# Decay series to the start, codes by GpSimd, two row sets by VectorE, unit splits to the end of the drain

## The chip, the cores and the metric

One core of a Trainium2 chip runs one layer of a decoder trunk for 256 tokens of 2048 features. The core has five engines, each with its own instruction queue, worked off in program order: TensorE (PE in the profile; its weight loads are PEld), VectorE (DVE), ScalarE (ACT), GpSimd (POOL) and SyncE (SP), which here only issues DMAs. An instruction waits at the head of its queue until what it needs is there, and everything behind it waits with it. The metric is the device time of one execution in microseconds, the median of the timed runs.

## The reference, cut to what matters

```python
z    = rmsnorm(h, norm1_g)
proj = z @ w_in                        # 1024 pool | 1024 x-branch | 1024 gate columns
xc   = causal depthwise conv4(x branch)
r, i = sigmoid(xc @ gate_a_w + b), sigmoid(xc @ gate_x_w + b)     # per head, 8 heads
log_a = (LRU_C * r) * log_sigmoid(lru_lambda)                     # the decay
a, b = exp(log_a), sqrt(-expm1(2 * log_a)) * (i * xc)
y    = concat(pool_mixer(pool columns), associative_scan(a, b) * gelu(gate))
h    = h + y @ w_out
# PEER: 8 heads, 16 of 128 x 128 = 16384 single-neuron experts each
z2   = rmsnorm(h, norm2_g);  q = z2 @ peer_wq
top 16 of (q . keys1) + (q . keys2)    # an expert's number is i1 * 128 + i2
act  = gelu(peer_u[expert] . z2);  w = softmax(top scores) * act
out  = rmsnorm(h + sum over the 128 chosen experts of w * peer_v[expert], norm_f_g)
```

## The kernel before, in words

**Stages.** Time runs through five of them. (1) Projections: `z` is transposed and normed, and 24 column blocks of `w_in` are multiplied, each followed over the next steps by its mixer work. (2) The output projection, the second norm and the queries. (3) The U stage: the first 1536 of the 2048 features are multiplied densely, all 16384 rows of `peer_u` by all 256 tokens, 64 pairs of row blocks with three units each; the scores stay on chip in `sw`. The last 512 features are gathered per chosen expert by GpSimd's indirect DMAs and dotted on VectorE. (4) The drain: for each token the 128 chosen scores are picked out of `sw` (extract), run through GELU and the softmax weights, and spread again into a 128 x 128 map of weights per token, written back into `sw` (form). (5) The V stage: the map times all rows of `peer_v`, densely for 1536 features, with gathers for the other 512; then residual and last norm.

**Units and splits.** Every weight comes in units of 128 x 1024 floats (512 KB). `Stream` (L68) holds them: `load` (L94) issues a unit's DMA on SP into a free raw buffer, `split` (L103) makes a high part on ScalarE (`hi`, L109) and the rest on VectorE (`lo`, L110), which frees the raw buffer, and `take` (L130) hands both to three matmuls per product (L359 to L361, L1107 to L1109). There are three raw and two high/low buffer pairs, more of either in some stages. `give_back` (L126) frees the pair used last.

**Projections and steps.** `Steps` (L138) is a plan by hand: `steps.at(k, f)` runs `f` k ticks later, two ticks to a column block. The plan at L336 to L344 sets the first norm, the splits of the gate weights and, at ticks 6, 8 and 9, the decay series. `decay_1` (L309) takes Abs and Exp of `lru_lambda`'s column on ScalarE, adds 2 on GpSimd and prepares four small rows of pooling divisors there (`inv`); `decay_2` (L317) takes two reciprocals on VectorE; `decay_3` (L321) sums a series of 27 GpSimd operations on 128 x 8 values and leaves the two scales `l8` and `l8n`, which are first used in `s10` (L433). GpSimd also computes `cl`, the low part of the convolved x branch (`pool_rest`, L261, called in `s4`, L411), which TensorE needs for the gate products in `s6` (L415).

**The drain.** The loop at L1116 runs n from 0 to 38 over groups of eight tokens, and its program order is the order on every engine. In iteration n it extracts group n (`extract_mm`, L987: code matmuls that mask by i2, then matmuls of the one-hot of i1 with `sw`; VectorE's maximum over 128 is the pick, L1001), forms group f = n - 6 (`form_mm`, L1064) and evacuates group f - 1 into `sw` on ScalarE (`form_out`, L1071). The one-hots of i1 for extracts (`onehot_t`, L870) come from GpSimd mostly, from index rows loaded by SP (`load_ib`, L866). A form needs two row sets of 8 x 128 per token group. `one` (L1029) is the one-hot of i1: on ScalarE eight Abs and a Relu (L1038, L1041), on VectorE one comparison (L1034); `O1_BY` and `O1_LAST` say which, the last six groups alternating ScalarE and VectorE. `two` (L1056) compares with i2 and multiplies by the weights on VectorE; `two_pool` (L1046) does one or two of the eight rows on GpSimd. Both sets have two buffers, so set k + 2 waits until form k has been read. The sets of the first groups go into unit buffers that are free by then (`early`, `early2`), and ScalarE builds the first three in iterations 0 to 2. Every fourth iteration runs a GELU over 32 tokens: VectorE (`gelu_1`), ScalarE's Square (`gelu_1s`, L1014), VectorE (`gelu_2`), ScalarE's Tanh (`gelu_2s`, L1023), VectorE (`gelu_3`, L1027), which writes the weights `wt`. The forms of a block cannot begin before that.

**Codes.** Before the extracts, tables of the chosen experts' i2 bits come back from DRAM: `code_tile` (L903) issues four DMAs of 8 KB on SP for two groups, three tiles ahead of the drain and the others inside it.

**The V stage's start.** At n = 9 the first three value units are loaded; at n = 14 and 18 (`V_SPLIT`) a unit is split and the next one loaded. At n = 33 and 34 TensorE does the first half of the products of value units 0 and 1 (`v_mm`, L1101).

Of the kernel before, what the change touches and what calls it, by code (L numbers as in the profile page):

```python
# [10 lines left out]
F32 = mybir.dt.float32  # L11
# [9 lines left out]
T = 256  # L21
# [27 lines left out]
NCB, V_LOAD, V_SPLIT = 3, 9, (14, 18)  # L49
# [109 lines left out]
def kernel(ctx: ExitStack, tc: tile.TileContext, x, cols, front, gates_w, keys, u1, u2, v1, v2,  # L159
# [60 lines left out]
    warm = cst.tile([128, 1], F32, name="warm")  # L220
    nc.vector.memset(warm, 1.0)
    nc.scalar.activation(warm, warm, AF.Sqrt)
    for c in range(4):
        if c == 2:
            st.load()
        for i in range(2):
            nc.sync.dma_start(xh[:, i, c * 512:(c + 1) * 512], x[i, :, c * 512:(c + 1) * 512])
    while st.load():
        pass
    graw = []  # L230
    for i in range(2):
        raw = fp.tile([128, 1024], F32, name="b8", tag="b8", bufs=3)
        nc.sync.dma_start(raw, gates_w[i])
        graw.append(raw)
    g2b = xpool.tile([128, D2], F32, name="g2b")
    gw = []

    nc.sync.dma_start(g2b, g2row.partition_broadcast(128))
    def split_gates(i):
        hi = fp.tile([128, 8, 128], F32R, name=f"gwh{i}")  # L240
        lo = fp.tile([128, 8, 128], F32R, name=f"gwl{i}")
        nc.scalar.activation(hi.rearrange("p a b -> p (a b)"), graw[i], AF.Copy)
        nc.gpsimd.tensor_tensor(lo.rearrange("p a b -> p (a b)"), graw[i],
                                hi.rearrange("p a b -> p (a b)").bitcast(F32), op=OP.subtract)
        gw.append((hi, lo))

    def rsqrt(dst, ss, scr):

        v, s, a = scr
        nc.vector.tensor_scalar(v, ss, 1.0 / D, EPS, op0=OP.mult, op1=OP.add)  # L250
        nc.scalar.activation(s, v, AF.Sqrt)
        nc.vector.reciprocal(s, s)
        nc.vector.tensor_tensor(a, s, s, op=OP.mult)
        nc.vector.tensor_tensor(a, a, v, op=OP.mult)
        nc.vector.tensor_scalar(a, a, -0.5, 1.5, op0=OP.mult, op1=OP.add)
        nc.vector.tensor_tensor(dst, s, a, op=OP.mult)

    def pool_mul(o, a, b):
        nc.gpsimd.tensor_tensor(o, a, b, op=OP.mult)

    def pool_rest(o, a, hi):  # L261
        nc.gpsimd.tensor_tensor(o, a, hi.bitcast(F32), op=OP.subtract)

    zhi, zlo = z_tiles()

    def to_z(k, srcs, gcol, zh, zl, p=None):

        p = bank("tp", 2) if p is None else p
        for i in range(2):
            nc.tensor.transpose(p[:, i * 128:(i + 1) * 128], srcs[i][:, k * 128:(k + 1) * 128], ident)  # L270
        nc.scalar.activation(zh[k], p[:, :T], AF.Copy, scale=gcol)
        nc.vector.scalar_tensor_tensor(zl[k], p[:, :T], gcol, zh[k].bitcast(F32), op0=OP.mult, op1=OP.subtract)

    def bcast_t(dst, v):

        p = bank("tp", 2)
        for i in range(2):
            nc.tensor.transpose(p[:, i * 128:(i + 1) * 128], v[:, i:i + 1].to_broadcast([128, 128]), ident)
        nc.scalar.activation(dst, p[:, :T], AF.Copy)

    def z1(k):
        tag, n = (("tp", 2), ("sm", 2), ("mm", 4), ("tp", 2), ("sm", 2), ("mm", 4), ("tp", 2), ("sm", 2))[k // 2]
        to_z(k, (xh[:, 0, :], xh[:, 1, :]), col("g1", k), zhi, zlo, bank(tag, n))


# [7 lines left out]
    jx = fp.tile([128, 2, D], BF, name="jx", tag="b8", bufs=3)[:, :, :512]  # L293
    ss1c = fp.tile([128, 2, 4], F32, name="ss1c")

    def square_x(c):
        cs = slice(c * 512, (c + 1) * 512)
        nc.scalar.activation(jx[:, 0, :], xh[:, 0, cs], AF.Square, accum_out=ss1c[:, 0, c:c + 1])
        nc.vector.scalar_tensor_tensor(jx[:, 1, :], xh[:, 1, cs], 1.0, xh[:, 1, cs], op0=OP.mult, op1=OP.mult,
                                       accum_out=ss1c[:, 1, c:c + 1])  # L300

    def first_norm():
        nc.vector.tensor_reduce(ss1, ss1c, AX.X, OP.add)
        rsqrt(rstd1, ss1, [fp.tile([128, 2], F32, name=f"rq{j}") for j in range(3)])
# [30 lines left out]

    steps.at(0, lambda: square_x(2))  # L336
# [5 lines left out]
    steps.at(6, decay_1)  # L342
    steps.at(8, decay_2)
    steps.at(9, decay_3)  # L344
# [567 lines left out]
    for pr in range(64):  # L912
        acc = [bank("mm", 4) for _ in range(2)]
        for kg in range(GU):
# [15 lines left out]
            if u == nu - DOT_END + 1:  # L930
# [5 lines left out]
                prepare_codes()  # L936
                ibt = zbpool.tile([128, 2, 8, 128], BF, name="ibt", tag="zbhi")
# [420 lines left out]
```

## Time and profile before

| | |
|---|---|
| median of 3 runs | 1629.93 us (1625.88 to 1631.35) |
| the profiled execution's own time | 1624.22 us |
| its span, first to last instruction | 1622.2 us |
| TensorE busy | 1570.7 us, 97% of the span |
| VectorE, GpSimd, ScalarE busy | 83%, 58%, 54% |
| projections to the end of queries | 0 to 340 us |
| U stage | 340 to 929 us, TensorE busy over 98% of it |
| drain | 929 to 1084 us, TensorE busy 139.75 of 155 us |
| V stage | 1084 to 1600 us, then the last norm |

Times inside an execution are microseconds from the span's start. A row of the timeline gives start, duration, engine, line, operation, tile written and tiles read, shapes and how many instructions were merged into it; in brackets stands how long the engine had been idle before it and what released it. The granted clock is a share of TensorE's full rate.

### The profile page before, as it was taken

How to read it: one execution, taken by the hardware profiler on the slowest of the kernel's cores; microseconds unless marked ns; L12 is line 12 of the kernel's file. 1: busy time of each engine (PE TensorE's matmuls, PEld its weight loads, DVE VectorE, ACT ScalarE, POOL GpSimd, SP SyncE). 2: the span in 40 equal slices, each digit the busy share in tenths (PEclk: the TensorE clock that was granted, in tenths of full speed). 3: DMA queues.
4: the chain of work that ended last, by engine and by line, in shares of the span. 5: the costliest groups of instructions: out<-in, count | busy, mean ns of one | idle time of the engine just before them, and what ended most of it. 6: DMA issues, size and time to landing. Idle time of an engine off the chain costs nothing.

```text
span 1622.2 us, 28967 instructions
## 1 busy us (share of the span) xinstructions
PE 1570.7 (97%) x10734; PEld 1452.3 (90%) x10734; DVE 1347.1 (83%) x2297; ACT 881.1 (54%) x1223; POOL 941.1 (58%) x754
## 2 busy tenths in 40 slices
PE   8899999999999999999999989989999999999996
PEld 8899888999999999999999989977888888888885
DVE  7799755899999998777777479978899898989897
ACT  6675545444444445444444568874555555555554
POOL 2476201266677778555554269866676666666663
PEclk9999999999999999999999999999999999999998
DMA  7455666578988889998998423129999999999992
GB/s 255 145 169 180 207 199 203 160 237 274 329 299 292 274 302 333 324 314 306 311 309 296 135 88 118 48 69 315 308 336 366 331 334 362 358 330 334 350 322 99
DMA packets 124973, 418.60 MB, mean 258 GB/s; under 512 B 18128, under 2 KB 20720, under 8 KB 124704
## 3 DMA queue, kind: packets, MB, share of 16 engines
q1 hardware_dynamic: 82528, 278.70, 52.2%
q0 software_dynamic: 42304, 138.06, 24.0%
q8 instruction: 84, 1.38, 0.4%
q14 instruction: 57, 0.47, 0.1%
HBM read 411.90 MB, written 4.78 MB: 257 GB/s over the span
## 4 chain that ended last, share of the span: by engine, by line
PE 76%; DVE 10%; ACT 6%; DMA 5%; issue 2%; POOL 1%; SPq 0%; ACTq 0%; DVEq 0%; POOLq 0%
PE mm L361 14%; PE mm L360 13%; PE mm L359 13%; PE acc L1108 9%; PE acc L1109 9%; PE acc L1107 9%; DVE lo L110 3%; DMA raw<-in_v_dram 2%; DVE sw L694 2%; PE mm L585 2%; PE mm L583 2%; PE mm L584 2%; ACT ott L1038 2%; DMA raw<-in_u_dram 1%; DVE sw L714 1%
## 5 line engine op out<-in xcount | busy, mean ns | idle before, releaser
L109 ACT ACTIVATE hi<-raw 128x1024 fp32r<-128x1024 f32 x390 | 413.1, 1059 | 470.9 <-PE mm L360 200.9
L110 DVE TENSOR_TENSOR lo<-raw,hi 128x1024 fp32r<-128x1024 f32 x390 | 495.4, 1271 | 176.6 <-ACT hi L109 171.7
L361 PE MATMUL mm<-zahi,lo 128*128 128x256 f32 x2016 | 572.6, 284 | 6.7 <-DVE lo L110 6.5
L359 PE MATMUL mm<-zahi,hi 128*128 128x256 f32 x2016 | 573.4, 284 | 0.0
L360 PE MATMUL mm<-zalo,hi 128*128 128x256 f32 x2016 | 571.3, 283 | 0.0
L1189 POOL DMA_INDIRECT gatv<-in_v_dram,e x256 | 327.0, 1277 | 179.4 <-DVE accg L1199 121.8
L361 PEld LDWEIGHTS mm<-zahi,lo 128*128 128x128 f32 x2016 | 387.5, 192 | 8.8 <-DVE lo L110 8.5
L359 PEld LDWEIGHTS mm<-zahi,hi 128*128 128x128 f32 x2016 | 387.8, 192 | 0.2
L360 PEld LDWEIGHTS mm<-zalo,hi 128*128 128x128 f32 x2016 | 387.7, 192 | 0.0
L684 POOL DMA_INDIRECT sw<-in_u_dram,e x128 | 160.6, 1254 | 90.9 <-DVE sw L694 39.1
L1107 PE MATMUL acc<-hi,wht 128*128 128x512 f32 x512 | 199.5, 390 | 1.7 <-ACT wht L1095 1.7
L1108 PE MATMUL acc<-lo,wht 128*128 128x512 f32 x512 | 199.7, 390 | 0.3 <-DVE lo L110 0.2
L1109 PE MATMUL acc<-hi,wlt 128*128 128x512 f32 x512 | 199.4, 389 | 0.0
L1199 DVE SCALAR_TENSOR_TENSOR accg<-gatv,wtok,accg 128x512 f32<-128x512 f32 x252 | 183.4, 750 | 3.3 <-DMA gatv<-in_v_dram,e 3.3
L1107 PEld LDWEIGHTS acc<-hi,wht 128*128 128x128 f32 x512 | 96.1, 188 | 21.9 <-ACT wht L1095 1.9
L1108 PEld LDWEIGHTS acc<-lo,wht 128*128 128x128 f32 x512 | 96.1, 188 | 21.7 <-DVE lo L110 1.9
L1109 PEld LDWEIGHTS acc<-hi,wlt 128*128 128x128 f32 x512 | 96.1, 188 | 20.0 <-DVE wlt L1096 0.4
L684 POOL DMA_INDIRECT gatp<-in_u_dram,e x64 | 74.2, 1160 | 55.9 <-DVE gatp L694 45.6
L684 POOL DMA_INDIRECT gatl<-in_u_dram,e x64 | 72.8, 1138 | 54.1 <-DVE gatl L694 43.4
L1108 PE MATMUL acc<-more,wht 128*128 128x512 f32 x256 | 100.1, 391 | 1.4 <-DVE more L110 1.4
L1107 PE MATMUL acc<-more,wht 128*128 128x512 f32 x256 | 99.7, 389 | 0.4 <-ACT more L109 0.4
L694 DVE SCALAR_TENSOR_TENSOR sw<-sw,zg 128x512 f32<-128x512 f32 x128 | 98.2, 786 | 2.0 <-DMA sw<-in_u_dram,e 2.0
(300 smaller groups left out, 2576.1 us busy)
## 6 DMA issues: line engine op xcount, KB each, us to landing
raw<-in_u_dram SPq DMA_DIRECT2D x192, 512.0 KB
raw<-in_v_dram SPq DMA_DIRECT2D x125, 512.0 KB
raw<-in_front_dram SPq DMA_DIRECT2D x114, 512.0 KB
sw<-in_v_dram SPq DMA_DIRECT2D x67, 512.0 KB
ibt<-i_dram SPq DMA_DIRECT2D x32, 256.0 KB
gatv<-in_v_dram,e POOLq DMA_INDIRECT x256, 5.9
xh<-in_x_dram SPq DMA_DIRECT2D x8, 256.0 KB
h_dram<-xh POOLq DMA_DIRECT2D x8, 256.0 KB, 4.7
```

The lines of the kernel that those rows point to most:

```text
L109: nc.scalar.activation(s[1], r[1], AF.Copy)
L110: nc.vector.tensor_tensor(s[2], r[1], s[1].bitcast(F32), op=OP.subtract)
L359: nc.tensor.matmul(o, ah, bh, start=first, stop=False)
L360: nc.tensor.matmul(o, ah, bl, start=False, stop=False)
L361: nc.tensor.matmul(o, al, bh, start=False, stop=last)
L684: nc.gpsimd.indirect_dma_start(out=g, out_offset=None, in_=u2, in_offset=bass.IndirectOffsetOnAxis(ap=e32[:, i, sl:sl + 1], axis=0))
L694: nc.vector.scalar_tensor_tensor(g, g, 1.0, zg[:, i, :], op0=OP.mult, op1=OP.mult, accum_out=sg[:, i, sl:sl + 1])
L1107: nc.tensor.matmul(banks[c][i], whi[:, j, ts], vh[:, s], start=first, stop=False)
L1108: nc.tensor.matmul(banks[c][i], whi[:, j, ts], vl[:, s], start=False, stop=False)
L1109: nc.tensor.matmul(banks[c][i], wlo[:, j, ts], vh[:, s], start=False, stop=last)
L1189: nc.gpsimd.indirect_dma_start(out=g, out_offset=None, in_=v2, in_offset=bass.IndirectOffsetOnAxis(ap=e32[:, i, s:s + 1], axis=0))
L1199: nc.vector.scalar_tensor_tensor(a, g, wtok[:, i, s:s + 1], a, op0=OP.mult, op1=OP.add)
```

## The change

- `decay_1` and `decay_2` are called before everything else that uses ScalarE and VectorE, ahead of the `warm` memset and its Sqrt (their definitions move up unchanged, with the tiles they use); `decay_3` is called once the first loads are issued. Ticks 6, 8 and 9 are empty of them.
- The first three code tiles are issued on GpSimd's queue, two right after their buffers are cleared (twelve units before the end of the U stage), the third after its own is cleared. Later tiles stay on SP.
- The row sets of groups 0 and 1 are compared on VectorE at the last unit of the U stage, where it already builds three sets of the other kind. ScalarE builds the third in iteration 0.
- The Square of the first GELU block is issued ahead of the extract of its iteration.
- From n = 32 on, ScalarE's row sets (28 and 30) are issued one iteration earlier, at n = 32 and n = 34.
- The two unit splits go from n = 14 and 18 to n = 33 and 35, after the last step of a GELU, and the first value products from n = 33 and 34 to 35 and 37.

```diff
-NCB, V_LOAD, V_SPLIT = 3, 9, (14, 18)
+NCB, V_LOAD, V_SPLIT = 3, 9, (33, 35)
...
     st.limit = n_v
+    lamc = colt[:, COLS["lam"]]
+    lt = [fp.tile([128, 8], F32, name=f"lt{j}") for j in range(4)]
...
+    decay_1()
+    decay_2()
     warm = cst.tile([128, 1], F32, name="warm")
     nc.vector.memset(warm, 1.0)
     nc.scalar.activation(warm, warm, AF.Sqrt)
...
     nc.sync.dma_start(g2b, g2row.partition_broadcast(128))
+    decay_3()
...
-    steps.at(6, decay_1)
-    steps.at(8, decay_2)
-    steps.at(9, decay_3)
...
-    def code_tile(k):
+    def code_tile(k, eng=nc.sync):
         for q in range(4 * k, min(4 * k + 4, T // 4)):
             g = q % 4
-            nc.sync.dma_start(code_buf[k % NCB][32 * g:32 * g + NCODE],
+            eng.dma_start(code_buf[k % NCB][32 * g:32 * g + NCODE],
...
                 prepare_codes()
+                code_tile(0, nc.gpsimd)
+                code_tile(1, nc.gpsimd)
...
                 nc.gpsimd.memset(code_buf[2], 0.0)
+                code_tile(2, nc.gpsimd)
             if u >= nu - 7 and st.loaded == n_v and not codes_out:
                 codes_out.append(u)
-                for k in range(NCB):
-                    code_tile(k)
                 for k in (2, 3):
                     load_ib(k)
             if u == nu - 1:
...
+                early = [by8(v) for e in (st.hl_free[0], st.hl[st.used - 1]) for v in e[1:]][:O1_EARLY]
+                for k in range(2):
+                    nc.vector.tensor_tensor(early[k], *rows(i1t, k), op=OP.is_equal)
...
         if gelu:
             gelu_1(b)
+            if b == 0:
+                gelu_1s(b)
...
-        g1s = (lambda: gelu_1s(b)) if gelu else lambda: None
+        g1s = (lambda: gelu_1s(b)) if gelu and b else lambda: None
         if 0 <= f + 1 < NP:
             two(f + 1)
-        if O1_EARLY <= f + 1 < NP:
+        by_act = lambda k: O1_LAST[k % 2] == "a"
+        if O1_EARLY <= f + 1 < NP and not (n > NP and by_act(f + 1)):
             one(f + 1, g1s)
         else:
             g1s()
+        if n >= NP and f + 2 < NP and by_act(f + 2):
+            one(f + 2)
...
-        if n < O1_EARLY:
-            one(n)
+        if n == 0:
+            one(O1_EARLY - 1)
...
+        if gelu:
+            gelu_3(b)
         if n in V_SPLIT:
             st.give_back()
             st.split()
             st.load()
-        if gelu:
-            gelu_3(b)
...
-        if n in (NP + 1, NP + 2):
-            c = n - NP - 1
+        if n in (NP + 3, NP + 5):
+            c = (n - NP - 3) // 2
             v_mm(0, c, 0, *st.hl[st.used + c][1:])
```

More of the change, by code (lines that the diff above doesn't have):

```diff
@@ L219 @@
     st.limit = n_v
[L220 to L283, printed above, removed]
     rstd1 = fp.tile([128, 2], F32, name="rstd1")
@@ L291, with pool_mul @@
     inv = fp.tile([128, 4, 16], F32, name="inv")
[L293 to L304, printed above, removed]
+    def pool_mul(o, a, b):
+        nc.gpsimd.tensor_tensor(o, a, b, op=OP.mult)
     lamc = colt[:, COLS["lam"]]
@@ L334, in decay_3 @@
         pool.tensor_scalar(l8n, lt[3], -LRU_C * 0.5, None, op0=OP.mult)
+    decay_1()
+    decay_2()
+    warm = cst.tile([128, 1], F32, name="warm")
+    nc.vector.memset(warm, 1.0)
+    nc.scalar.activation(warm, warm, AF.Sqrt)
+    for c in range(4):
+        if c == 2:
+            st.load()
+        for i in range(2):
+            nc.sync.dma_start(xh[:, i, c * 512:(c + 1) * 512], x[i, :, c * 512:(c + 1) * 512])
+    while st.load():
+        pass
+    graw = []
+    for i in range(2):
+        raw = fp.tile([128, 1024], F32, name="b8", tag="b8", bufs=3)
+        nc.sync.dma_start(raw, gates_w[i])
+        graw.append(raw)
@@ new lines, in rsqrt, with pool_rest @@
+    def rsqrt(dst, ss, scr):
+        v, s, a = scr
+        nc.vector.tensor_scalar(v, ss, 1.0 / D, EPS, op0=OP.mult, op1=OP.add)
+        nc.scalar.activation(s, v, AF.Sqrt)
+        nc.vector.reciprocal(s, s)
+        nc.vector.tensor_tensor(a, s, s, op=OP.mult)
+        nc.vector.tensor_tensor(a, a, v, op=OP.mult)
+        nc.vector.tensor_scalar(a, a, -0.5, 1.5, op0=OP.mult, op1=OP.add)
+        nc.vector.tensor_tensor(dst, s, a, op=OP.mult)
+    def pool_rest(o, a, hi):
+        nc.gpsimd.tensor_tensor(o, a, hi.bitcast(F32), op=OP.subtract)
@@ new lines, with to_z, bcast_t @@
+    zhi, zlo = z_tiles()
+    def to_z(k, srcs, gcol, zh, zl, p=None):
+        p = bank("tp", 2) if p is None else p
+        for i in range(2):
+            nc.tensor.transpose(p[:, i * 128:(i + 1) * 128], srcs[i][:, k * 128:(k + 1) * 128], ident)
+        nc.scalar.activation(zh[k], p[:, :T], AF.Copy, scale=gcol)
+        nc.vector.scalar_tensor_tensor(zl[k], p[:, :T], gcol, zh[k].bitcast(F32), op0=OP.mult, op1=OP.subtract)
+    def bcast_t(dst, v):
+        p = bank("tp", 2)
+        for i in range(2):
+            nc.tensor.transpose(p[:, i * 128:(i + 1) * 128], v[:, i:i + 1].to_broadcast([128, 128]), ident)
+        nc.scalar.activation(dst, p[:, :T], AF.Copy)
@@ new lines, in z1, with square_x @@
+    def z1(k):
+        tag, n = (("tp", 2), ("sm", 2), ("mm", 4), ("tp", 2), ("sm", 2), ("mm", 4), ("tp", 2), ("sm", 2))[k // 2]
+        to_z(k, (xh[:, 0, :], xh[:, 1, :]), col("g1", k), zhi, zlo, bank(tag, n))
+    jx = fp.tile([128, 2, D], BF, name="jx", tag="b8", bufs=3)[:, :, :512]
+    ss1c = fp.tile([128, 2, 4], F32, name="ss1c")
+    def square_x(c):
+        cs = slice(c * 512, (c + 1) * 512)
+        nc.scalar.activation(jx[:, 0, :], xh[:, 0, cs], AF.Square, accum_out=ss1c[:, 0, c:c + 1])
+        nc.vector.scalar_tensor_tensor(jx[:, 1, :], xh[:, 1, cs], 1.0, xh[:, 1, cs], op0=OP.mult, op1=OP.mult,
+                                       accum_out=ss1c[:, 1, c:c + 1])
@@ L336, with first_norm @@
+    def first_norm():
+        nc.vector.tensor_reduce(ss1, ss1c, AX.X, OP.add)
+        rsqrt(rstd1, ss1, [fp.tile([128, 2], F32, name=f"rq{j}") for j in range(3)])
     steps.at(0, lambda: square_x(2))
@@ L973 @@
     o1s, o2s = (ott[:, 0], ott[:, 1]), (ott[:, 2], ohtt[:, 2])
-    early = [by8(v) for e in (st.hl_free[0], st.hl[st.used - 1]) for v in e[1:]][:O1_EARLY]
     def o1(n, read=False):
```

10 lines of the change are left out of this document (added).

## The prediction

> **What bounds the kernel now.** I read the times by stage first, then what TensorE (PE) waited for, then the three stages that the change touches in order of time. Columns of the stretches: length, busy time of each engine with its instructions, granted clock, DMA share, GB/s.
>
> ```profile
> 50.00:55.30 5.30, 0.36 (x4) 0.16 (x2) 2.70 (x5) 1.06 (x1) 4.54 (x13) 0.72 0.65 191
> 55.30:59.20 3.90, 3.85 (x18) 3.86 (x19) 1.36 (x3) 1.44 (x3) 1.37 (x2) 0.51 0.04 14
> 948.00:952.20 4.20, 4.13 (x24) 4.13 (x24) 3.61 (x5) 0.00 (x0) 4.08 (x2) 0.50 0.23 70
> 1010.00:1057.00 47.00, 44.72 (x422) 43.31 (x421) 44.82 (x51) 39.50 (x96) 36.31 (x14) 1.00 0.20 54
> 1057.00:1084.00 27.00, 19.56 (x157) 17.91 (x156) 20.56 (x26) 20.66 (x43) 17.24 (x13) 1.00 0.00 1
> 1160.00:1600.00 440.00, 440.00 (x1941) 363.76 (x1940) 397.32 (x440) 231.68 (x218) 279.02 (x220) 1.00 0.94 331
> ```
>
> PE sets the end: in the long value stage (1160 to 1600) it is never idle, so what is saved ahead of that stage moves the end by as much, unless its loads come too late. It stands still at few places; the waits are total, times, longest:
>
> ```profile
> PE tp L360 <- POOL cl L262: 5.0, 1, 5.0
> PE exb L991 <- DVE asw L1001: 4.8, 1, 4.8
> ```
>
> ```profile
> PE fob L1067 <- ACT ott L1041: 4.0, 4, 1.7
> PE fob L1067 <- DVE ott L1034: 3.9, 2, 2.0
> ```
>
> One is in the projection near 50 us, three are in the drain (929 to 1084). After each of the first two the clock is granted at half (0.51, 0.50) for some 4 us. The drain's last part is a chain between four engines, none of them full.
>
> **The change part by part.** Sums go against the profiled execution: 1624.22 us, its span 1622.2. It lies 5.7 us under the median of the timed runs; I carry the difference over to the median, 1629.93.
>
> *Decay series, gain near 50 us.* The wait of 5.0 us is TensorE wanting `cl` from GpSimd, and GpSimd does the series first:
>
> ```profile
> 54.25 0.23 POOL L334 TENSOR_SCALAR l8n<-lt 128x8 f32<-128x8 f32 x1
> 54.57 1.41 POOL L262 TENSOR_TENSOR cl<-xc,ch 128x256 fp32r<-128x256 f32 x2
> ```
>
> Moved away, `cl` no longer queues behind it. The stall goes, and with it the slow clock: 3.9 us at half rate are 18 matmuls, which at full rate (0.12 us against 0.21 start to start) take 2.2, so 1.7 more. **-6.7 us.** Next late could be ScalarE: its table load moves to the first gate's Tanh (48 us).
>
> ```profile
> 47.34 1.06 ACT L109 ACTIVATE hi<-raw 128x1024 fp32r<-128x1024 f32 x1 [1.29 <-issue]
> ```
>
> The split ahead of it had waited 1.29 us, so I cost it at nothing; uncovered it is 1.28 (the load's row comes with the start). The series itself then runs on GpSimd where it has nothing else until 28.9 us, and its two results are first used past 55 us.
>
> *Decay series, cost at the start.* The first z evacuation waits for the column constants (5.90) and ScalarE has its Sqrt table by then:
>
> ```profile
> 5.90 0.84 ACT L271 ACTIVATE zahi<-tp,colt 128x256 fp32r<-128x256 f32 x2 [3.68 <-DMA colt<-in_cols_dram]
> ```
>
> ```profile
> 11.46 1.23 DVE L110 TENSOR_TENSOR lo<-raw,hi 128x1024 fp32r<-128x1024 f32 x1 [0.46 <-ACT hi L109]
> ```
>
> Now there stands between: Abs and Exp on ScalarE (0.2 each), five small GpSimd operations, two VectorE reciprocals, the `warm` memset behind these in VectorE's queue, and the Sqrt that waits for it.
>
> ```profile
> 35.25 2.33 POOL L315 TENSOR_SCALAR inv<-iota 128x16 f32<-128x16 f32 x4
> ```
>
> ```profile
> 33.42 1.28 ACT L312 ACT_TABLE_LOAD   x1
> 34.71 0.21 ACT L312 ACTIVATE lt<-lt 128x8 f32<-128x8 f32 x1
> ```
>
> Four of the five took 2.33 us beside a busy VectorE; small ones like L334 above take 0.23, so 0.9 to 2.3, and with VectorE idle I take 1.2. 0.4 + 0.25 + 1.2 + some 0.5 of reciprocals and memset + 0.3 of hand-overs = 2.7 us, so z starts at 8.6. The second table switch (1.28, from 6.3 to 7.6) hides behind the reciprocals. Of the 2.7, 1.3 are absorbed, since ScalarE waited that long before its fifth z:
>
> ```profile
> 8.73 0.90 ACT L271 ACTIVATE zahi<-mm,colt 128x256 fp32r<-128x256 f32 x2 [1.26 <-PE mm L270]
> ```
>
> The first unit's `lo` and all matmuls behind it come **+1.4 us** later (0.5 to 2.7; 4 if every GpSimd operation takes its slow form).
>
> In the Trainium skill, "ScalarE: Activation LUTs", section "What ACT_TABLE_LOAD costs", a switch is 1.28 us and a drain of 1.38. Here the Exp starts 0.01 us after the load ends, so no drain shows; by the page the switch would end at 9.0 and the term be about 1.9.
>
> *Codes by GpSimd.* Twelve issues; the nearest row is a small load on that queue:
>
> ```profile
> L808 POOL DMA_DIRECT2D wtok<-in_code_dram x4 | 2.1, 550 | 0.0
> ```
>
> ```profile
> 928.77 2.85 POOL L881 TENSOR_SCALAR oht<-ibt,pidx 128x1024 f32<-128x1024 bf16 x1 [19.66 <-PE mm L361]
> ```
>
> 12 x 0.55 = 6.6 us, out of 19.7 that GpSimd waited for the end of the U stage; what is queued behind them, the first two one-hots, is wanted only then. So nothing, up to some 1.6 us an issue. SP gives up twelve issues late in the U stage, when its unit loads are all out: nothing.
>
> *Two row sets by VectorE.* VectorE has the time: it does 2 x 1.2 us in the 3.4 it waits for the first extract.
>
> ```profile
> 931.92 1.23 DVE L1001 TENSOR_REDUCE asw<-exb 128x8 f32<-128x1024 f32 x1 [3.36 <-PE exb L996]
> ```
>
> ScalarE loses two row sets of 3.5 us each ahead of the first GELU:
>
> ```profile
> 940.33 2.43 ACT L1038 ACTIVATE hi<-iota,late 128x128 fp32r<-128x128 f32 x8
> 942.79 1.06 ACT L1041 ACTIVATE hi<-hi 128x1024 fp32r<-128x1024 f32 x1
> 943.75 1.13 ACT L878 ACTIVATE oht<-ibt,pidx 128x1024 f32<-128x1024 bf16 x1
> 944.92 1.06 ACT L879 ACTIVATE oht<-oht 128x1024 f32<-128x1024 f32 x1
> 945.88 0.21 ACT L1014 ACTIVATE tv<-tv 128x32 f32<-128x32 f32 x1
> ```
>
> ```profile
> 938.10 4.65 SPq L868 DMA_DIRECT2D ibt<-i_dram  x2
> ```
>
> ```profile
> 948.07 1.01 PE L991 MATMUL exb<-asw,i1f 128*128 128x128 bf16 x8 [4.83 <-DVE asw L1001]
> ```
>
> Seven us earlier would be 938.9, but the one-hot ahead of the GELU (943.75) needs its indices, issued by SP at 938.10 and not moved; such a load took 3.2 us from issue to use:
>
> ```profile
> 930.25 6.36 SPq L868 DMA_DIRECT2D ibt<-i_dram  x3
> ```
>
> ```profile
> 933.42 2.85 POOL L881 TENSOR_SCALAR ohta<-ibt,pidx 128x1024 f32<-128x1024 bf16 x1 [1.80 <-DMA ibt<-i_dram]
> ```
>
> So that one-hot starts at 941.3, the GELU's Square at 943.4 instead of 945.88, and PE's wait shrinks from 4.8 to 2.4. Stops of up to 2.0 us later in the drain leave the clock at 1.00 (row 1057 to 1084), stops of 4.8 and 5.0 halved it; I take 2.4 to be too short, which gives back 2.4 us more, worked from eight code matmuls, 16 extracts and part of a form at half rate (4.3 + 2.2 us against 2.3 + 1.8). **-4.8** (-2.4 if the clock falls all the same). Issuing the first Square ahead of the extract changes nothing: ScalarE has nothing between.
>
> *Splits out of the middle.* They were here, with VectorE full (44.82 of 47 us):
>
> ```profile
> 989.09 1.22 DVE L110 TENSOR_TENSOR lo<-raw,hi 128x1024 fp32r<-128x1024 f32 x1
> ```
>
> ```profile
> 1007.63 1.25 DVE L110 TENSOR_TENSOR lo<-raw,hi 128x1024 fp32r<-128x1024 f32 x1 [1.82 <-ACT hi L109]
> ```
>
> The first held VectorE for 1.1, the second with its wait 3.0: 4.1 at most. PE limits that: it is busy for 44.72 of the 47 us from 1010 on, so 2.3 are to be had there and somewhat more around the second split, ahead of 1010. Between, **-3.3** (-2.3 to -4.1).
>
> *Splits and one-hots in the last iterations.* In clock times of before:
>
> ```profile
> 1067.02 0.23 ACT L1023 ACTIVATE tv<-tv 128x32 f32<-128x32 f32 x1 [2.99 <-DVE tv L1018]
> ```
>
> ```profile
> 1078.22 2.05 PE L1067 MATMUL fob<-ott 128*128 128x128 f32 x16 [1.36 <-ACT ott L1041]
> 1080.11 1.95 PE L1067 MATMUL fob<-oht,ott 128*128 128x128 f32 x16
> 1081.90 0.27 PE L1075 MATMUL fob<-ident,asw 128*128 128x128 f32 x1
> 1083.87 0.50 PE L1107 MATMUL acc<-hi,wht 128*128 128x512 f32 x1 [1.69 <-ACT wht L1095]
> ```
>
> At n = 32 row set 28 fills ScalarE's idle 2.99 us, from 64.6 to 68.1, but the last Tanh (67.02) queues behind it: last weights at 68.5 instead of 67.3. GpSimd's two scaled rows, which need the weights,
>
> ```profile
> 1067.64 3.27 POOL L1050 TENSOR_SCALAR ott<-iota,late,asw 128x128 f32<-128x128 f32 x2 [4.40 <-DVE asw L1027]
> ```
>
> end at 71.9, and form 28 starts there, as before (71.6). At n = 34 row set 30 waits for form 28 to end (74.0) and runs until 77.5; form 28's evacuation, 1.0 us, now stands behind it: 78.5. Only then can the second split's `hi` run (79.5), and its `lo` on VectorE, which has idled since 76.9, ends at 80.8. Behind that `lo` are three operations for form 31 (0.95, 1.05, 1.2): 84.0, and form 31 starts there instead of 80.1. Behind it in PE's queue are the first half of value unit 1 (1.5 us) and the token transpose; then ScalarE's copies. The value stage starts at 88.9 instead of 83.9: **+5.0** (+2 to +8). That the first split takes ScalarE and VectorE at n = 33 is inside these clock times.
>
> The two next unit loads are issued at 71.7 and 80.8, where DMA was idle (0.00); their units are needed at 92 or later: nothing.
>
> Sum: -6.7 + 1.4 - 4.8 - 3.3 + 5.0 = **-8.4 us**: 1615.8 for an execution like the profiled one, **1621.5** on the median.
>
> **Rivals.**
> (1) *The last chain goes cold.* PE would idle from 68.4 to 71.9 and from 80.5 to 84.0, 3.5 us each, between the 2.0 that kept the clock and the 4.8 that lost it. At the price near 50 us (1.7 each) that is +3.4: 1624.9. In the Trainium skill, "TensorE: Matmul & The Clock Gate", section "What's actually happening", the clock falls after an idle window of about 3.4 us: by that rule 2.4 us at the drain's start stays warm, and these two stops are just on the line.
> (2) *The drain's start stays cold after 2.4 us*: +2.4, 1623.9. For it speaks only that a stop remains.
> (3) *The tail is cheaper*, if the second `hi` slips ahead of form 28's evacuation in time (row set 30 not late): then VectorE loses only two times 1.2 us less its old waits of 1.8, about +1 instead of +5: 1617.5. Against it: program order on ScalarE is fixed.
> (4) *The start costs what it returns*: slow GpSimd forms, +4 to +5 instead of 1.4: about 1624.8.
> (5) *Value loads exposed, slower*: value units 3 and 4 were in memory by 1010; now they come with the first gathers. In that stage the chain goes through loads like this one:
>
> ```profile
> 1096.04 7.54 DMA raw<-in_v_dram
> ```
>
> If both cost their whole time, 15.1 us, it is 1636.6; from 8.4 us on (a load that lands after its split is wanted by over 4.2 us) the change is a loss. Against it: the value stage has DMA share 0.94 with PE never idle, and both issues come ahead of the gathers.
> (6) *Next late near 50 us*: table load and units queue behind each other and 1.3 of the 6.7 stays: 1622.8, inside the first case.
>
> **How the numbers follow.** About 0.3% (4.9 us) is what a measurement of this kernel can tell; faster is below 1625.0. Forecast with (6) 0.52, (1) 0.15, (2) 0.08, (3) 0.11, (4) 0.08, (5) 0.06. Forecast and (3) are faster nearly whole, of (1), (2) and (4) half, since they lie on the bound: 0.72. Slower takes (5) and a remainder: 0.07; 0.21 for no change. Range: lowest, the tail at +1, all of 4.1 from the middle and a start of +0.5: -14.0, 1615.9; highest, a start of +4 and a tail of +8: -2.8, 1627.1; and 2 to 3 us on either side, since the three runs themselves lie 5.5 apart: 1613 to 1629.
>
> **What would show it.** No wait for `cl` near 50 us and clock 1.00 from 55 to 60; the first z on ScalarE near 8.6 and the first `lo` near 12.9; PE's wait for the fifth pick at about 2.4 us with no half clock after it; iterations of 4.1 us through 980 to 1057; in the last iterations VectorE waiting 2 to 3 us for the second split's `hi`, and 5 us more from form 26 to the value stage. I am wrong if the last chain is no longer than before, or if PE waits for raw value units after it.

## The result and the profile after

The changed kernel takes 1617.02 us, median of five runs (1614.05 to 1618.78). The kernel before takes 1629.69 beside it (1624.08 to 1631.35). The ratio is 0.993, with an interval of 0.9914 to 0.9946: 8.8 to 14.0 us faster. The forecast was 1621.5, in the range 1613 to 1629. Measured by the medians the gain was 12.7 us and not 8.4, and two of its terms came out quite differently from how they were worked out.

The profiled execution of the changed kernel is the slowest of its five: own time 1618.78, span 1617.0. That of before was near the fastest of its runs (1624.22, 1622.2). The two spans therefore show less than the medians do. I compare by stages below, over all traces.

Stretches of the changed kernel (length, busy time and instructions of PE, PEld, VectorE, ScalarE, GpSimd, granted clock, DMA share, GB/s):

```profile
50.00:55.30 5.30, 5.30 (x47) 5.30 (x46) 4.02 (x8) 4.89 (x9) 1.49 (x2) 1.00 0.51 128
55.30:59.20 3.90, 3.90 (x36) 3.90 (x34) 3.47 (x6) 3.90 (x9) 1.35 (x2) 1.00 0.67 206
947.70:952.00 4.30, 4.30 (x45) 4.29 (x45) 4.26 (x5) 0.06 (x1) 4.07 (x2) 1.00 0.28 58
989.00:1037.00 48.00, 47.36 (x462) 46.72 (x461) 46.40 (x51) 41.75 (x100) 48.00 (x19) 1.00 0.24 72
1063.50:1065.40 1.90, 1.72 (x9) 1.43 (x8) 1.86 (x3) 1.55 (x3) 1.90 (x2) 0.50 0.00 0
1160.00:1600.00 440.00, 439.98 (x1942) 364.12 (x1940) 395.63 (x437) 231.32 (x222) 281.23 (x219) 1.00 0.93 327
```

Near 50 us PE is now full at full clock, where it had 0.36 of 5.30 us and half clock behind it. The clock is also full after the first picks (third row). GpSimd is busy for all of the 48 us in the middle of the drain. A half clock has appeared in the tail (1063.5). The value stage is as full as before.

What PE waited for, changed kernel (total, times, longest):

```profile
PE mm L362 <- DVE lo L110: 10.4, 12, 1.9
...
PE fob L1070 <- DVE ott L1037: 3.2, 2, 2.0
PE fob L1070 <- POOL ott L1053: 2.4, 3, 1.2
PE exb L994 <- DMA i2f<-code_dram: 2.4, 1, 2.4
...
PE fob L1070 <- ACT ott L1044: 1.4, 2, 0.7
```

The wait for `cl` is gone. The 4.8 for the fifth pick has become 2.4, and the view now names a transfer for it. That name is wrong: the pick itself (L1004) is what ends then.

```profile
943.80 1.15 ACT L879 ACTIVATE oht<-ibt,pidx 128x1024 f32<-128x1024 bf16 x1 [2.94 <-DMA ibt<-i_dram]
...
946.40 1.22 DVE L1004 TENSOR_REDUCE asw<-exb 128x8 f32<-128x1024 f32 x1
...
947.67 0.61 PE L994 MATMUL exb<-asw,i1f 128*128 128x128 bf16 x8 [2.37 <-DMA i2f<-code_dram]
```

946.40 + 1.22 = 947.62, and PE goes on at 947.67. The named transfer fills `i2f`; the row reads `i1f`, whose transfers were issued 7.5 us earlier or more.

The table shows where the time went, stage by stage. Each column is the distance between two starts in the trace: from 0 to the first product of the output projection, from the first key product to the first code product (the U stage), from there to the last extract, from there to the first value product behind the last token (the tail), and from there to the last group of three value products. All in us.

```
                     to output   U stage   first code to   tail   value stage
                    projection              last extract
before                 171.2      648.6        130.4       24.1      523.6
before, again          170.8      654.3        131.2       24.1      519.5
changed                164.5      657.2        123.8       26.1      521.0
changed, again         164.7      645.5        124.4       26.1      523.2
decay only             164.9      653.3        129.5       24.1      522.4
rows only              170.9      654.2        126.3       24.1      521.1
splits back            165.4      653.6        127.4       23.1      520.3
splits back, again     166.3      648.4        128.3       23.1      522.1
one-hots late          166.6      651.6        122.3       31.0      520.1
one GpSimd row         165.4      660.1        124.7       26.9      521.5
codes by SP            165.2      653.2        123.8       26.1      521.4
start freed            163.9      652.2        124.0       26.1      520.1
start and splits       164.9      651.2        127.4       23.1      520.4
splits apart           166.5      649.3        125.5       24.9      524.8
```

The U stage takes 648.6 and 654.3 us in two executions of one program, and 645.5 and 657.2 in two of the other. So a single span can't be compared to better than some 10 us. The three stages that the change touches repeat to 1 or 2 us, and the tail to 0.1. Three of the expectations below (splits back, the first time; one-hots late; one GpSimd row) give this tail as 27.9 us: they count from the code products of the last group, 1.8 us before its last extract product, where the table's 26.1 begins.

### The profile page after: what moved, and what is told of

Same layout as the page of the kernel before. It is cut to its first block, busy times and chain, and to the rows that moved or that the text cites. A ratio compares the mean times of both kernels' runs of the same rounds, so it can differ in the third digit from the quotient of the medians.

```text
span 1617.0 us, 28964 instructions
## 1 busy us (share of the span) xinstructions
PE 1570.9 (97%) x10734; PEld 1453.1 (90%) x10734; DVE 1355.6 (84%) x2299; ACT 874.0 (54%) x1206; POOL 953.1 (59%) x766
## 3 DMA queue, kind: packets, MB, share of 16 engines
q8 instruction: 84, 1.38, 0.4%
## 4 chain that ended last, share of the span: by engine, by line
PE 74%; DVE 10%; DMA 5%; ACT 5%; issue 3%; POOL 3%; another core or an unknown queue 0%; ACTq 0%; POOLq 0%; DVEq 0%; SPq 0%
PE mm L362 12%; PE mm L361 12%; PE mm L360 12%; PE acc L1111 10%; PE acc L1112 10%; PE acc L1110 10%; DVE lo L110 3%; DVE sw L695 2%; DMA raw<-in_u_dram 2%; PE mm L586 2%; PE mm L585 2%; PE mm L584 2%; ACT ott L1041 1%; ACT hi L109 1%; DVE sw L715 1%
## 5 line engine op out<-in xcount | busy, mean ns | idle before, releaser
L110 DVE TENSOR_TENSOR lo<-raw,hi 128x1024 fp32r<-128x1024 f32 x390 | 499.7, 1282 | 173.6 <-ACT hi L109 152.4
L1197 POOL DMA_INDIRECT gatv<-in_v_dram,e x256 | 333.7, 1304 | 169.6 <-DVE accg L1207 111.9
L685 POOL DMA_INDIRECT sw<-in_u_dram,e x128 | 156.1, 1220 | 103.7 <-DVE sw L695 45.8
L1112 PE MATMUL acc<-more,wlt 128*128 128x512 f32 x256 | 99.6, 389 | 0.0
```

Source lines behind the costliest of these rows:

```text
L110: nc.vector.tensor_tensor(s[2], r[1], s[1].bitcast(F32), op=OP.subtract)
L685: nc.gpsimd.indirect_dma_start(out=g, out_offset=None, in_=u2, in_offset=bass.IndirectOffsetOnAxis(ap=e32[:, i, sl:sl + 1], axis=0))
L1112: nc.tensor.matmul(banks[c][i], wlo[:, j, ts], vh[:, s], start=False, stop=last)
L1197: nc.gpsimd.indirect_dma_start(out=g, out_offset=None, in_=v2, in_offset=bass.IndirectOffsetOnAxis(ap=e32[:, i, s:s + 1], axis=0))
```

## The experiments

**Decay only.** The kernel before, with only the decay series moved to the beginning.

> The kernel before with the decay series at the start and nothing else. Theory (separate gains): by the trace of the changed kernel TensorE's wait of 5.0 us for cl and the half clock after it go, the start costs some 0.5 us, and the whole time falls by 6 us (ratio 0.996), because what the U stage took more in the profile of the changed kernel is spread between executions. Rival (given back): the U stage takes up what the projections gain, as the profile of the changed kernel looks (output projection 6.6 us earlier, end of the U stage 2.1 us later): ratio 1.000 or above, and the stretch from the first key product to the last U unit is longer by 6 us or more. The prediction's own terms said -6.7 + 1.4 = -5.3.

```
+    decay_1()
+    decay_2()
     warm = cst.tile([128, 1], F32, name="warm")
...
     nc.sync.dma_start(g2b, g2row.partition_broadcast(128))
+    decay_3()
...
-    steps.at(6, decay_1)
-    steps.at(8, decay_2)
-    steps.at(9, decay_3)
```

1614.67 us against 1624.71, ratio 0.9933 (0.9907 to 0.9959). The output projection starts at 164.9, so 5.9 to 6.3 us earlier than in the two traces of before. The first `lo` on VectorE shows what the start cost. Its times are 11.46 and 11.32 before, and in the kernels with the early series 12.48 here, 12.05 in the earliest and 13.12 in the latest of those that keep the start as changed; the column constants land at different moments. Timeline of this kernel, then of the kernel before run again:

```profile
6.18 1.28 ACT L264 ACT_TABLE_LOAD   x1
8.39 0.20 ACT L264 ACTIVATE warm<-warm 128x1 f32<-128x1 f32 x1 [0.92 <-DVE up L355]
8.50 0.82 ACT L312 ACTIVATE zahi<-tp,colt 128x256 fp32r<-128x256 f32 x2
...
12.48 1.23 DVE L110 TENSOR_TENSOR lo<-raw,hi 128x1024 fp32r<-128x1024 f32 x1 [0.27 <-ACT hi L109]
```

```profile
11.32 1.23 DVE L110 TENSOR_TENSOR lo<-raw,hi 128x1024 fp32r<-128x1024 f32 x1 [0.46 <-ACT hi L109]
```

From the first `lo` to the output projection it is 159.4 to 159.7 us without the early series (three traces) and 152.4 to 153.7 with it (nine): the wait and its half clock were worth 5.8 to 7.3 us, the start cost 0.6 to 1.8. The rival, that the gain is given back in the U stage, falls: 653.3 us there lies between the two traces of before, and the whole time gained 10.0 us (6.7 to 15.1). The stage gained 6 of them; what the other 4 are, no stage of the trace shows. By whole times alone this edit could not be told from the whole change (0.993).

**Rows only.** The kernel before, with only the two early row sets done by VectorE.

> The kernel before with the row sets of groups 0 and 1 on VectorE at the last U unit and the third on ScalarE in iteration 0, nothing else. Theory: TensorE's wait for the fifth pick falls from 4.8 to 2.4 us, the clock stays full after it, and the first form starts 4.5 us sooner after the first extract than in the kernel before (there 23.0 us); of that some is lost at the two splits in the middle, where VectorE is full: whole time -3 to -5 us, ratio 0.997 to 0.998. Rival (clock falls all the same): only 2.4 us sooner, granted clock 0.5 for 4 us after the wait, ratio 0.999.

```
             if u == nu - 1:
...
+                early = [by8(v) for e in (st.hl_free[0], st.hl[st.used - 1]) for v in e[1:]][:O1_EARLY]
+                for k in range(2):
+                    nc.vector.tensor_tensor(early[k], *rows(i1t, k), op=OP.is_equal)
...
-        if n < O1_EARLY:
-            one(n)
+        if n == 0:
+            one(O1_EARLY - 1)
```

1621.55 us, ratio 0.9979 (0.9966 to 0.9992): 1.3 to 5.5 us faster. PE's longest wait in the drain is halved:

```profile
PE exb L992 <- DVE asw L1002: 2.7, 1, 2.7
```

From the first code to the last extract it takes 126.3 us, against 129.5 to 131.2 in three traces without it: 3.2 to 4.9 less, with 4.8 worked out. The clock stayed full behind the stop in this trace, so the rival did not happen here; the first form starts 18.8 us after the first code product, against 23.0 before.

**Splits back.** The changed kernel with both unit splits back in the middle of the drain, run on two chips, the second time beside the changed kernel itself.

> The changed kernel with the two unit splits back at n = 14 and 18 and the first value products at n = 33 and 34. Theory (tail bound by GpSimd's scaled rows, which are slow beside VectorE's splits): from the last extract to the first product of the value stage proper 24 to 26 us instead of 27.9, the iterations from the eighth to the last extract 2 to 4 us longer than 101.3; whole time within 2 us of the changed kernel. Prediction's step (the splits' place itself: -3.3 in the middle, +5.0 in the tail): 1.7 us faster than the changed kernel. Rival (the splits' move is the gain): slower than the changed kernel by 4 us or more.

```
-NCB, V_LOAD, V_SPLIT = 3, 9, (33, 35)
+NCB, V_LOAD, V_SPLIT = 3, 9, (14, 18)
...
-        if n in (NP + 3, NP + 5):
-            c = (n - NP - 3) // 2
+        if n in (NP + 1, NP + 2):
+            c = n - NP - 1
```

> The changed kernel with both unit splits back in the middle of the drain, once more, on one chip with the changed kernel. Theory (the move costs as much in the tail as it saves in the middle): the tail is 3.0 us shorter (23.1), the middle 1.5 to 3.4 us longer (106.8), the time 0 to 1.5 us under that of the changed kernel beside it. Rival 1, the prediction's sum (5.0 lost, 3.3 saved): 1.7 us faster, with a tail 5 us shorter. Rival 2 (the move is a gain, since every engine is full in the middle): 2 us slower than the changed kernel.

> The changed kernel itself, as the yardstick for the three beside it. Every theory: output projection at 164.5 to 165.4 us, last extract to first value product 26.1 us, ratio to before 0.993 to 0.995. What is open is the stretch from the first form to the last extract: 105.2 us in its first trace, 103.4 in three variants that touch nothing there. Theory (chance, a place in a sequence of waits): 103 to 106 again. Rival (something of the program): 105.2 again, to 0.3 us. The clock: the stop at the first pick is 2.4 to 2.8 us and the clock after it is either full, then 18.5 to 19 us from the first code product to the first form, or half for some 4 us, then 20.3 to 21.3; it was full in four of six traces with such a stop.

First 1613.62 us, ratio 0.9924 (0.9894 to 0.9954). Then 1612.58 (1611.22 to 1615.41), against 1611.85 (1610.01 to 1618.67) of the changed kernel beside it; before was 1624.43 there, and the ratios are 0.993 (0.9915 to 0.9945) and 0.9933 (0.9914 to 0.9952). Moving the splits makes no difference that these runs can tell. The stages show why: in these pairs, what it saves and costs differ by less than 1 us. In the tail the splits cost 26.1 - 23.1 = 3.0 us. In the middle they cost 127.4 - 123.8 = 3.6, or 128.3 - 124.4 = 3.9 with the second pair, and this is what the move saves. Over all traces, with no split in the middle (122.3 to 124.7) and with two (127.4 to 128.3), the middle's figure is less sure: 2.7 to 6.0. So the saving was near what was worked out (3.3), the cost was not (5.0).

The second trace of the changed kernel also settled the clock behind the first picks. Its stretches and timeline there:

```profile
937.80:939.80 2.00, 2.00 (x13) 2.00 (x12) 2.00 (x3) 0.00 (x0) 2.00 (x2) 0.50 0.00 0
939.80:941.80 2.00, 2.00 (x18) 2.00 (x18) 2.00 (x3) 0.00 (x0) 2.00 (x1) 0.93 0.44 147
```

```profile
933.30 1.15 ACT L879 ACTIVATE oht<-ibt,pidx 128x1024 f32<-128x1024 bf16 x1 [4.01 <-DMA ibt<-i_dram]
...
937.16 1.01 PE L994 MATMUL exb<-asw,i1f 128*128 128x128 bf16 x8 [3.45 <-DVE asw L1004]
```

The same program, and here ScalarE waits 4.01 us for its indices instead of 2.94. PE stops for 3.45 instead of 2.37, and the clock is at half for some 3 us. Even so, it takes 124.4 us to the last extract, against 123.8 with the full clock. From the first form to the last extract the second trace takes 103.4 us and the first 105.3. So the first gives its lead back there, in part where a form's last two products wait for GpSimd:

```profile
985.18 0.49 PE L1070 MATMUL fob<-ott 128*128 128x128 f32 x2 [0.91 <-POOL ott L1053]
```

It need not. One-hots late, the next variant, is the same program up to the last extract. Its clock was full as well, and it kept its lead: 103.4 us from the first form, 122.3 in all.

**One-hots late.** The changed kernel with ScalarE's row sets of the last iterations back where they were, the splits left in the tail.

> The changed kernel with ScalarE's row sets 28 and 30 issued in their old iterations. If the early sets serve the tail, its forms 28 and 30 wait for ScalarE again (about 1.7 and 1.4 us in the kernel before): last extract to value stage 29 to 31 us instead of 27.9, whole time +1 to +3 us. If GpSimd's scaled rows bound the tail whatever ScalarE does: 27.9 within 0.7 us, whole time unchanged.

```
-        if O1_EARLY <= f + 1 < NP and not (n > NP and by_act(f + 1)):
+        if O1_EARLY <= f + 1 < NP:
             one(f + 1, g1s)
...
-        if n >= NP and f + 2 < NP and by_act(f + 2):
-            one(f + 2)
```

1616.73 us, ratio 0.9949 (0.9932 to 0.9966), and a tail of 31.0 us instead of 26.1. In that tail PE waited for (total, times, longest):

```profile
PE fob L1070 <- DVE ott L1037: 6.6, 3, 2.5
PE fob L1070 <- ACT ott L1044: 3.8, 2, 3.1
```

```profile
1061.96 3.28 PE L1070 MATMUL fob<-ott 128*128 128x128 f32 x16 [3.08 <-ACT ott L1044]
1062.89 1.22 DVE L110 TENSOR_TENSOR lo<-raw,hi 128x1024 fp32r<-128x1024 f32 x1 [3.09 <-ACT hi L109]
...
1070.71 1.23 DVE L110 TENSOR_TENSOR lo<-raw,hi 128x1024 fp32r<-128x1024 f32 x1 [1.59 <-ACT hi L109]
```

PE waits 3.08 us for ScalarE's row set 28. The splits' `hi` stand behind the row sets on ScalarE, and VectorE waits 3.09 and 1.59 us for them, with all of its later rows behind. Counted as in the expectation the tail is 32.8 us, more than the 29 to 31 there. So the early row sets are worth 4.9 us where the splits stand in the tail. Where they don't, they are worth 24.1 - 23.1 = 1.0.

**One GpSimd row.** The changed kernel with one instead of two scaled rows per form on GpSimd in the last iterations; VectorE takes the other.

> The changed kernel with one scaled row on GpSimd instead of two for the last six groups (VectorE takes the other). Theory (GpSimd's rows, 2.1 us each there, bound the tail): GpSimd ends some 7 us sooner, TensorE's waits for it in the tail (2.1 us in all) go, and from last extract to value stage it takes 25 to 27 us instead of 27.9. Rival (VectorE is the bound, back to back for 13 us from the last weights to row set 31): it gets 0.27 us more per group, the tail 28 to 29.5 us.

```
-O2_POOL, O2_POOL_LAST = (1, 0), 2
+O2_POOL, O2_POOL_LAST = (1, 0), 1
```

1619.72 us, ratio 0.994 (0.9923 to 0.9957); the tail is 26.9 us, 0.8 longer. In the tail, PE's waits and two of its forms:

```profile
PE fob L1070 <- DVE ott L1037: 3.6, 3, 2.5
PE fob L1070 <- DVE ott L1065: 0.9, 1, 0.9
```

```profile
1074.87 3.75 PE L1070 MATMUL fob<-oht,ott 128*128 128x128 f32 x16 [0.65 <-DVE ott L1037]
...
1082.33 2.02 PE L1070 MATMUL fob<-oht,ott 128*128 128x128 f32 x16 [0.41 <-DVE ott L1037]
```

No wait for GpSimd is left, and the tail is no shorter. The last form (1082.33) starts when VectorE's last operation ends. VectorE works from 1063.28 to there, 19 us, with a gap of 0.74 as its longest; in the changed kernel the same work took it 17.6. Two forms ran at half clock here (3.75 us), but beside VectorE's work. The theory that GpSimd alone holds the tail falls: counted as in the expectation it is 28.7 us, as the rival had it. But in the changed kernel VectorE does not hold it alone either. There GpSimd's scaled rows run back to back from 1063.45 to 1078.14, PE's last wait for a row set (1.22 us) is for them, and form 31 starts 0.96 after VectorE is done. The two engines end so close together that moving this row from one to the other gained nothing.

**Codes by SP.** The changed kernel with the codes loaded by SP, as before.

> The changed kernel with all code tiles on SP as before. By the prediction the twelve issues are hidden on either queue: no change of the whole time (within 0.3%), first extract no earlier and no later against the end of the U stage. If GpSimd's issues matter, its first two one-hots end 4 us sooner and the drain's start moves; if SP's matter, the third and fourth index load come 4 us later and the first one-hot on ScalarE waits for them: +1 to +3 us.

```
                 prepare_codes()
-                code_tile(0, nc.gpsimd)
-                code_tile(1, nc.gpsimd)
...
-                code_tile(2, nc.gpsimd)
...
                 codes_out.append(u)
+                for k in range(NCB):
+                    code_tile(k)
```

1617.48 us, ratio 0.9939 (0.9923 to 0.9956). All stages agree with the changed kernel's to 0.7 us except the U stage with its spread. That part of the change does nothing, as forecast.

**The kernel before, again.** One run, for a second trace of it.

> The kernel before once more, for a second trace. Theory (U stage differs between executions of one program): projections and drain agree with the first trace within 0.5 us, the stretch from the first key product (280.6) to the first extract (929.4) is not 648.8 again but differs by 2 to 8 us, TensorE's waits for lo in it between 5 and 12 us. Rival (it is a fixed property of each kernel): 648.8 within 1 us.

1626.27 us. It gave the second line of the table, without which the U stage's 8.6 us between the first two traces would have looked like a cost of the change. The two traces of before differ by 5.7 us there, as the theory had it; the rival, 648.8 us again, falls.

**Start freed.** The changed kernel with the divisors and both reciprocals taken out of the way of the Sqrt table.

> The changed kernel with the warm memset first on VectorE, the four rows of pooling divisors after the series and their reciprocal at tick 6, so that between the column constants and the first z only Abs, Exp, table load and Sqrt are left. By the changed kernel's trace the first z then starts 0.9 us sooner (1.9 instead of 2.8 after Abs), the first matmul that needs lo 0.3 to 0.4 us sooner, and the whole time is the same. If the start's chain costs what the prediction said (1.4), it is 1 us sooner there.

```
+    warm = cst.tile([128, 1], F32, name="warm")
+    nc.vector.memset(warm, 1.0)
     decay_1()
-    decay_2()
-    warm = cst.tile([128, 1], F32, name="warm")
-    nc.vector.memset(warm, 1.0)
...
+    decay_2()
     decay_3()
+    divisors()
...
+    steps.at(6, lambda: nc.vector.reciprocal(inv, inv))
```

1616.83 us, ratio 0.9934 (0.9917 to 0.995). Its timeline:

```profile
6.15 1.28 ACT L264 ACT_TABLE_LOAD   x1
...
7.44 0.20 ACT L264 ACTIVATE warm<-warm 128x1 f32<-128x1 f32 x1
7.55 0.82 ACT L314 ACTIVATE zahi<-tp,colt 128x256 fp32r<-128x256 f32 x2
...
11.54 1.22 DVE L110 TENSOR_TENSOR lo<-raw,hi 128x1024 fp32r<-128x1024 f32 x1 [0.27 <-ACT hi L109]
```

From the table load to the first `lo` it is now 5.39 us, against 6.30 above: 0.9 us gained. That is under what a time can show here.

**Start and splits**, both edits together, and **splits apart**, the first split in the middle and the second in the tail.

> The changed kernel with the splits back in the middle and with the decay series' divisors and reciprocals taken out of the chain ahead of the first table load. Theory: output projection near 164 us (0.6 to 1 us earlier), tail 23.1, so 1 to 2.5 us faster than the changed kernel, ratio to before near 0.992. Rival (the first loads of the units set the start, not ScalarE's chain): output projection at 164.5 to 165.4 as in the changed kernel and no gain beside the splits'.

> The changed kernel with the first split in the middle (iteration 14) and the second in the tail (iteration 35). Theory (VectorE is full in both places and each split takes its own 1.2 to 1.5 us wherever it stands): tail 24.5 us, middle 1 to 1.5 us longer than in the changed kernel beside it, time within 1 us of it. Rival (the second split's wait for ScalarE, not VectorE's own work, costs in both places): one split in the tail costs 0.5 or less (23.6) and one in the middle 1.1, so 1.5 to 3 us faster than either.

```
-NCB, V_LOAD, V_SPLIT = 3, 9, (33, 35)
+NCB, V_LOAD, V_SPLIT = 3, 9, (14, 35)
```

1612.26 us (0.9925; 0.991 to 0.994) and 1616.0 (0.9937; 0.9918 to 0.9957), on the same chip as the two of 1611.85 and 1612.58. None of the four can be told from the others. With start and splits the output projection comes at 164.9, as in the changed kernel and not near 164, and no time is gained, as the rival had it. With one split in each place, the tail is 24.9 (1.8 over none, 1.2 under two), so the rival of one almost free split (23.6) falls. The way to the last extract is 125.5: 0.8 to 3.2 over none, 1.9 to 2.8 under two. So a split costs 1.2 to 1.8 us in the tail and some 1 to 3 in the middle, at least about its own 1.2 on VectorE in both. That agrees with the theory, though the middle's figures are too spread to show it there. No version was found that beats the changed kernel.

## Why the prediction was right, and where it was not

*Decay near 50 us, -6.7:* right. Full clock and no wait; 5.8 to 7.3 us in the traces. ScalarE's table load, costed at nothing there, left little: between 13 and 170 us the largest group of PE's waits is 1.1 us or less in every trace with the early series.

*Start, +1.4 (0.5 to 2.7):* right, 0.6 to 1.8. The working holds too: the four slow GpSimd operations took 1.27 (1.2 taken), and the load began right behind the Exp. Changed kernel, start:

```profile
5.55 0.21 ACT L236 ACTIVATE lt<-lt 128x8 f32<-128x8 f32 x1
5.78 1.28 ACT L264 ACT_TABLE_LOAD   x1
...
6.08 1.27 POOL L239 TENSOR_SCALAR inv<-iota 128x16 f32<-128x16 f32 x4
...
7.39 0.55 DVE L243 RECIPROCAL inv<-inv 128x64 f32<-128x64 f32 x1 [1.04 <-POOL inv L239]
...
7.98 0.20 ACT L264 ACTIVATE warm<-warm 128x1 f32<-128x1 f32 x1 [0.92 <-DVE up L355]
8.09 0.82 ACT L312 ACTIVATE zahi<-tp,colt 128x256 fp32r<-128x256 f32 x2
```

The first z comes at 8.1 here and at 9.1 in the latest of the nine traces (8.6 forecast). By the figures of the Trainium skill, "ScalarE: Activation LUTs", section "What ACT_TABLE_LOAD costs", a drain of 1.38 us would have come on top of the switch. With the start freed, the next activation runs 0.01 us behind the end of the load, so no drain shows there either.

*Codes by GpSimd, 0:* right.

*Two row sets, -4.8:* the stage's gain is about right (3.2 to 4.9 alone), but one of its two halves stood on a wrong step. The wait shrank to 2.37 us for the reason given. That "2.4 is too short" for the clock to fall is not a rule of this kernel. In the eleven traces that have this shorter stop it lasts 2.4 to 3.7 us, since the index load comes at different times, and the clock was full behind it in four (stops of 2.4 to 2.8) and at half in seven (2.6 to 3.7). So what rival (2) named happened in most of them. What it costs lies between nothing and 2.4 us: the six traces without a split in the middle take 122.3, 123.8 and 124.0 us to the last extract with the full clock, and 123.8, 124.4 and 124.7 with half.

*Splits out of the middle, -3.3:* right, 3.6 and 3.9 in the two pairs, 2.7 to 6.0 over all traces.

*Splits and one-hots in the last iterations, +5.0:* wrong. It was 26.1 - 24.1 = +2.0. This is the main miss, and it is a wrong step, not a wrong size. I had row set 30 on ScalarE wait for form 28 to end, since both use one buffer; form 28's evacuation, the second `hi` and `lo`, and form 31 were to queue behind that. Changed kernel, tail:

```profile
1063.45 4.33 POOL L1053 TENSOR_SCALAR ott<-iota,late,asw 128x128 f32<-128x128 f32 x2 [4.72 <-DVE asw L1030]
...
1065.42 2.10 PE L1070 MATMUL fob<-ott 128*128 128x128 f32 x14 [0.20 <-DVE ott L1065]
1066.22 2.54 ACT L1041 ACTIVATE ott<-iota,late 128x128 f32<-128x128 f32 x8
...
1067.83 0.49 PE L1070 MATMUL fob<-ott 128*128 128x128 f32 x2 [0.31 <-POOL ott L1053]
...
1070.66 1.05 ACT L109 ACTIVATE hi<-raw 128x1024 fp32r<-128x1024 f32 x1
1071.74 1.23 DVE L110 TENSOR_TENSOR lo<-raw,hi 128x1024 fp32r<-128x1024 f32 x1 [0.47 <-ACT hi L109]
...
1074.80 1.21 DVE L1037 TENSOR_TENSOR ott<-iota,late 128x1024 f32<-128x1024 f32 x1
...
1076.64 0.49 PE L1070 MATMUL fob<-ott 128*128 128x128 f32 x2 [1.22 <-POOL ott L1053]
1076.97 1.95 PE L1070 MATMUL fob<-oht,ott 128*128 128x128 f32 x16
```

Row set 30 starts at 1066.22, while form 28 still has products to do. The set is eight instructions of one slice each, and each waits only for the products that read its slice. For the same reason form 28 starts its first 14 products before GpSimd's second row is there, which I had gate the whole form. Nothing is late on ScalarE, VectorE waits 0.47 us for the second `hi` and not 2 to 3, and it is busy nearly without a gap until 1076.01. Row set 28 was misjudged in the same way: the last weights come 0.3 us later than before, counted from the last extract, and not 1.2. What remains is work. VectorE is done 20.8 us after the last extract, against 18.3 with the splits back, which is two times the 1.23 of a `lo`; GpSimd's rows end 2.4 later too, and form 31 starts at 21.8 instead of 19.4. The other 0.6 of the splits' 3.0 us lies behind form 31, where the first products of value unit 1 now stand. The early row sets give 1.0 back. This is near rival (3), +1 instead of +5, though its reason was another: it thought of the second `hi` slipping ahead.

*Rival (1), a cold last chain:* it happened in a smaller form. The two stops of 3.5 us did not come, yet the clock fell to half at 1063.5 behind a stop of 1.97 us:

```profile
1062.02 3.19 PE L1070 MATMUL fob<-oht,ott 128*128 128x128 f32 x16 [1.97 <-DVE ott L1037]
```

The second trace has the same stop and keeps the clock there (the form takes 2.02 us, not 3.19); it loses it 7.5 us later behind a stop of 1.23:

```profile
1050.99 2.02 PE L1070 MATMUL fob<-oht,ott 128*128 128x128 f32 x16 [1.97 <-DVE ott L1037]
...
1058.52 3.23 PE L1070 MATMUL fob<-oht,ott 128*128 128x128 f32 x16 [1.23 <-DVE ott L1037]
```

The tail is 26.1 us in both, so neither fall cost anything here.

*Value loads (rival 5):* did not happen. PE waits for no raw unit, and the value stage takes 521.0 and 523.2 us, against 523.6 and 519.5.

*The sum.* To the output projection it is 4.2 to 6.6 us less in the nine traces with the early series as changed, 5.5 in the mean (5.3 forecast). From the first code to the value stage it is 149.9 and 150.4 against 154.5 and 155.3, so 4.7 (3.1 forecast). Together that is 10.2 us, inside the measured 8.8 to 14.0. That it comes so near the 8.4 forecast is in part luck: the tail costs 3.0 us less than forecast, and the way to the last extract saves 1.4 less (6.7 instead of 8.1). The 2.5 us between it and the medians' 12.7 no stage of the traces accounts for, and the spread of the U stage is large enough to hide them; this stays open. One slip of the working: the lowest end of the range adds up to -14.1 and not -14.0, which changes nothing.

## What to carry to other kernels

Follow a shared buffer slice by slice before letting one instruction wait for another: an operation written as eight instructions starts eight times. In a stage where every engine is full, moving work from one place to another moves its cost along; ask which engine has a gap. Profile the old kernel twice before reading a stage's difference: here one stage alone spread by more than the whole gain.

## What the hardware showed that I had not expected

No length of a stop separates full from half clock here. Stops of 2.4 to 2.8 us before the first picks left it full four times, one of 2.6 and two of 2.8 did not, and in the tail 1.97 us was once followed by half clock and once not. "TensorE: Matmul & The Clock Gate" in the Trainium skill, section "What's actually happening", has a window of about 3.4 us that runs freely. That place in the window decides agrees with one program giving both outcomes. That a whole idle window is needed does not agree with a fall behind 1.97 us, a stop with shorter ones on either side.

GpSimd's scaled rows slow down beside a busy VectorE: two took 4.17 us (from 1067.76) to 4.67 (from 1071.92), but 1.56 once VectorE had stopped at 1076.01. Changed kernel, tail:

```profile
1067.76 4.17 POOL L1053 TENSOR_SCALAR oht<-iota,late,asw 128x128 f32<-128x128 f32 x2
...
1071.92 4.67 POOL L1053 TENSOR_SCALAR ott<-iota,late,asw 128x128 f32<-128x128 f32 x2
...
1076.58 1.56 POOL L1053 TENSOR_SCALAR oht<-iota,late,asw 128x128 f32<-128x128 f32 x2
```

The Trainium skill, "SBUF — State Buffer", section "SBUF: two separate sides", says that VectorE operations with two inputs from SBUF and GpSimd operations that read SBUF lock a shared pair of ports against each other. VectorE's work in that stretch is of that kind, and the rows agree. So work given to GpSimd to relieve VectorE costs it up to three times its price where VectorE is full.
